# Scores of both softmax maps in one three-bank tile, and a third bank in the rotation of the other attention matmuls

## The chip, the cores and the metric

The kernel runs on one core of one Trainium2 chip. The engines named here are TensorE (PE, with its weight loads shown apart as PEld), VectorE (DVE), ScalarE (ACT), GpSimd (POOL) and SyncE (SP), whose queue issues the DMAs. Each engine takes its instructions in order; semaphores hold an instruction back until what it depends on is done. Matmul results go into accumulator tiles in PSUM. A tile of 128 x 512 f32 is called a bank here; the kernel's PSUM pools hold eight of them at any time.

The metric is the time of one execution on the device, in microseconds (us).

## The reference

Two layers of a trunk over 512 latent and 256 context tokens of width 1024. In each layer both streams are normalised and modulated, projected once into the inputs of a convolution branch, of an attention branch (q, k, v) and of two gates, merged, projected back, and passed through an MLP. What matters here is the differential attention, eight heads with two softmax maps each:

```python
def block(qi):
    s = jnp.einsum('bqhcd,bkhcd->bhcqk', qi, keys) * scale      # c: the two maps
    p = jax.nn.softmax(s, axis=-1)
    w = p[:, :, 0] - lam * p[:, :, 1]
    return jnp.einsum('bhqk,bkhv->bqhv', w, vals)
```

Latent queries (four tiles of 128 tokens) see all 768 keys. Context queries (two tiles, in the first layer only) see the 256 context keys. All products are made from operands split into a rounded part and a remainder, so that most matmuls come in threes (lines 107 to 109), and those of the scores in twos.

## The kernel before, in words

The layers run one after the other. A layer's attention loops over eight heads. While head h is attended (`attend`), the projections of head h + 1 (`qk_head`) and a share of the values of the next pair of heads (`v_pair`) are filled in between; with the last head it is the convolution's projections (`conv_a`, `conv_g`). `merge` lays the two streams out in one program order by estimated costs. The framework then sorts each engine's instructions by a timeline of its own (line 1356), so that in the trace matmuls of several steps lie among each other.

`attend` does this for each token tile t (`scores`, lines 680 to 723): for map 0 and then map 1, matmuls into a score tile S; a reduce on DVE for the row maximum (L707); an exp on ACT with that maximum as its bias (L710) into `e0` or `e1`. `e0` has two buffers, `e1` one. Then a few small instructions and L720, which combines both maps into `e0`. Later `turn` transposes the combined weights on PE (`wT`, L733) and splits them on ACT and DVE; `values` multiplies them with the values (`av`), `finish` takes the sum of squares (L758).

`qk_head` has its own steps: `project` (24 matmuls into an `mm` tile, read by an ACT copy, L537), normalisation and rotation on DVE and POOL, and `turn` (four transposes into another `mm` tile, read by L579 on ACT and by L580 and L582 on DVE). In the last layer context queries are not needed, so the context keys go another way: `ctx_keys` (kc), `ctx_norm` (kcT) and `ctx_turn` (kcD), one `mm` tile each. `v_pair` takes an `mm` tile for each of six token tiles (`v`), read by ACT and DVE (L76, L77). `conv_a` and `conv_g` take them too (`ca`, `cg`).

PSUM during attention: pool `psA` with two banks for all `mm` tiles (line 73), pool `psS` with two S tiles of two banks each (768 of 1024 columns used by a latent tile, 256 by a context tile), pool `psX` with one bank for `wT` and one for `av`. A tile takes its pool's buffers in turn, and its first writer waits until the last reader of the tile before in that buffer is done. Ahead of a layer's attention, and of the gates that follow, other pools lie in the same six banks.

Of the kernel before, what the change touches and what calls it, by code (L numbers as in the profile page):

```python
# [8 lines left out]
F32 = mybir.dt.float32  # L9
# [5 lines left out]
P = 128  # L15
# [36 lines left out]
def trunk_kernel(  # L52
# [6 lines left out]
    nc = tc.nc  # L59
    PSUM = bass.MemoryType.PSUM  # L60
# [9 lines left out]


    def mm_tile(name):
        return psA.tile([P, 512], F32, tag="mm", name=name)

    def split(hi, lo, src, lo_eng=None):
# [60 lines left out]
    rs_d = [dpool.tile([H, SEQ if i == DEPTH - 1 else NT], F32, name=f"rs_d{i}")  # L136
            for i in range(DEPTH)]

    state = {"behind": ()}
    both = nc.vector, nc.gpsimd  # L140
    first = {}

# [287 lines left out]
    for i in range(DEPTH):  # L430
# [12 lines left out]
        apool = tc.tile_pool(name=f"apool{i}", bufs=2, reuse_waits="tile")  # L443
# [230 lines left out]
        def attend(h):  # L674

            QH, QL = QKt[h]
# [3 lines left out]
            def scores(t):  # L680
                u, j = t // 2, t % 2
                lat = u < 2
                nk, kb = (NTT, 0) if lat else (2, 4)
                nkey = nk * P
                if j == 0:
# [4 lines left out]
                                     bufs=3) for tg in ("wth", "wtl")] for g in range(ng)],  # L690
                        es2=ap.tile([P, 2], F32, tag="es2", name=f"es2{i}_{h}_{u}"))
                nm = f"{i}_{h}_{t}"
                ts = slice(t * P, t * P + P)
                es = []
                st = ap.tile([P, 8], F32, tag="st", name=f"st{nm}", bufs=4)
                for m in range(2):
                    S = pS.tile([P, 768], F32, tag="S", name=f"S{nm}_{m}")
                    for lo, hi in ((0, 512), (512, 768)):
                        lo = max(lo, kb * P)
                        if hi <= lo:  # L700
                            continue
                        o = slice(lo - kb * P, hi - kb * P)
                        nc.tensor.matmul(S[:, o], QH[:, m, ts], QH[:, 2 + m, lo:hi],
                                         start=True, stop=False)
                        nc.tensor.matmul(S[:, o], QL[:, m, ts], QH[:, 2 + m, lo:hi],  # L705
                                         start=False, stop=True)
                    nc.vector.tensor_reduce(out=st[:, m : m + 1], in_=S[:, :nkey], axis=AX.X,  # L707
                                            op=ALU.max, negate=True)
                    e = ap.tile([P, 768], F32, tag=f"e{m}", name=f"e{m}{nm}", bufs=2 - m)
                    nc.scalar.activation(out=e[:, :nkey], in_=S[:, :nkey], func=AF.Exp,  # L710
                                         bias=st[:, m : m + 1],
                                         accum_out=st[:, 2 + m : 3 + m])
                    es.append(e)
# [77 lines left out]
        def spill_rstd():  # L791

            n = H * qt_n
            ps = mm_tile(f"rsT{i}")
            nc.tensor.transpose(ps[:n, :P], rsall, ident)
            row = spool.tile([P, 4, P], F32, tag="dg", name=f"rst{i}", bufs=1)[:, 0]
            nc.vector.tensor_copy(row[:n], ps[:n, :P])
            nc.sync.dma_start(rs_d[i].rearrange("h (t p) -> (h t) p", p=P), row[:n])
            yield 0.5

        def drain(gen):
            for _ in gen:
                pass
# [66 lines left out]
        turn_tile = None  # L870
        for pl in early:
            pl.__exit__(None, None, None)
        pspool = tc.tile_pool(name=f"psS{i}", bufs=2, space=PSUM, reuse_waits="tile")
        pS = pspool.__enter__()
        psx = tc.tile_pool(name=f"psX{i}", bufs=1, space=PSUM, reuse_waits="tile")
        pX = psx.__enter__()
        att_cost = 23.03 if last else 27.37
# [23 lines left out]
                main = chain_(main, rest_of(carry))  # L901
            merge(main, chain_(*fill), fc / att_cost)
        drain(spill_rstd())
        for pl in (psx, pspool, apool):
            pl.__exit__(None, None, None)


# [181 lines left out]
        for s in range(2):  # L1089
# [7 lines left out]
            for m in range(4):  # L1097
# [9 lines left out]
                for g in groups:  # L1107
                    rr[g.start] = gp.tile([P, 512], F32, tag="ar", bufs=3,
                                          name=f"mr{i}_{mb}_{g.start}")[:, : g.stop - g.start]
# [251 lines left out]
```

## Time and profile before

| | us |
|---|---|
| median of 3 runs (2361.84 to 2371.28) | 2370.24 |
| the profiled execution's time | 2368.32 |
| its span | 2366.5 |
| PE busy in the span | 2286.9 |
| first layer's attention, in the trace | 86 to 493 |
| second layer's attention, in the trace | 1440 to 1795 |

The page sorts the span of one execution by engine, by slices of time, by the chain that ended last and by groups of instructions. Matmuls are written with the tile that they make and the tiles that they read, without buffer numbers: `S<-qk` is a score matmul, `e<-S,st` an exp, `v` a values tile. "x <- y: total, times, longest" in the waits means that x's engine stood idle until y was done. The granted clock is a share of TensorE's full 2.4 GHz; its other level is 1.2 GHz.

### The profile page before, as it was taken

The page shows a single profiled execution, that of the slowest core. Times are in us where ns is not written, and L with a number is a line of the kernel's source. Part 1 is how long each engine was busy: PE and PEld are TensorE (multiplying, and loading weights), DVE is VectorE, ACT ScalarE, POOL GpSimd, SP SyncE. Part 2 cuts the span into 40 slices and gives each one's busy share as a digit, 9 for nine tenths or more (in the row PEclk, how much of TensorE's full clock was granted, in tenths as well). Part 3 has the DMA queues.
Part 4 walks back from the last instruction along what each step waited for, and adds up shares of the span by engine and source line. Part 5 has one row for each costly group of instructions (what it writes and reads, how often), then busy time and mean ns, then how long its engine had stood idle before and what let it go on. Part 6 is the DMA issues. An engine that isn't in the chain of part 4 may idle for free.

```text
span 2366.5 us, 36536 instructions
## 1 busy us (share of the span) xinstructions
PE 2286.9 (97%) x14698; PEld 2049.6 (87%) x14698; DVE 1477.9 (62%) x2581; ACT 992.1 (42%) x1965; POOL 689.4 (29%) x792
## 2 busy tenths in 40 slices
PE   7999999999999999999999998999999999999999
PEld 6999998888888988888888997999877879888887
DVE  6777776699666665555563366676759976433333
ACT  5555654522332353242514345555542333532432
POOL 2866754100000133232232365766610000000000
PEclk9999999999999999999999999999999999999999
DMA  9211111144535223334332211111123324232322
GB/s 306 60 43 35 44 45 44 46 159 135 173 114 186 84 81 124 117 115 133 108 112 85 90 55 56 43 43 41 43 76 126 129 88 127 82 97 92 104 89 71
DMA packets 222570, 224.76 MB, mean 95 GB/s; under 512 B 6256, under 2 KB 212544, under 8 KB 222272
## 3 DMA queue, kind: packets, MB, share of 16 engines
q1 hardware_dynamic: 222400, 222.43, 29.2%
q8 instruction: 115, 1.88, 0.3%
q14 instruction: 55, 0.45, 0.1%
HBM read 208.73 MB, written 13.67 MB: 94 GB/s over the span
## 4 chain that ended last, share of the span: by engine, by line
PE 81%; DVE 10%; DMA 3%; ACT 3%; POOL 2%; issue 1%; SPq 0%; ACTq 0%; DVEq 0%; POOLq 0%
PE r L107 6%; PE r L108 6%; PE r L109 6%; PE f L108 6%; PE f L107 6%; PE f L109 5%; PE gt L107 3%; PE gt L109 3%; PE gt L108 3%; PE qk L107 2%; PE qk L108 2%; PE qk L109 2%; PE v L107 2%; DVE adaac L261 2%; PE v L108 2%; PE v L109 2%
## 5 line engine op out<-in xcount | busy, mean ns | idle before, releaser
L108 PE MATMUL f<-h2l,h_w 128*128 128x512 f32 (+1 forms) x832 | 284.0, 343 | 3.8 <-DVE h2l L326 2.0
L107 PE MATMUL r<-fh,h_w 128*128 128x512 f32 (+1 forms) x832 | 283.9, 342 | 0.4 <-DVE X L1135 0.4
L107 PE MATMUL f<-h2h,h_w 128*128 128x512 f32 (+1 forms) x832 | 282.3, 343 | 2.0 <-ACT h2h L76 1.3
L108 PE MATMUL r<-fl,h_w 128*128 128x512 f32 (+1 forms) x832 | 283.2, 340 | 0.1
L109 PE MATMUL r<-fh,l_w 128*128 128x512 f32 (+1 forms) x832 | 282.9, 340 | 0.0
L109 PE MATMUL f<-h2h,l_w 128*128 128x512 f32 (+1 forms) x832 | 282.5, 341 | 0.0
L77 POOL TENSOR_TENSOR l_w<-r_w,h_w 128x1024 fp32r<-128x1024 f32 x64 | 158.1, 2492 | 348.4 <-ACT h_w L76 348.4
L261 DVE SCALAR_TENSOR_TENSOR adaac<-ar,cvec,adaac 128x256 f32<-128x256 f32 x336 | 183.0, 597 | 89.3 <-DMA ar<-in_w_ada_dram 64.2
L76 ACT ACTIVATE h_w<-r_w 128x1024 fp32r<-128x1024 f32 x128 | 128.5, 1051 | 261.5 <-PE r L108 117.2
L940 DVE SCALAR_TENSOR_TENSOR cacc<-z,cols,cacc 128x783 f32<-128x783 f32 (+1 forms) x240 | 201.1, 890 | 0.3
L107 PE MATMUL qk<-h_wqk,h1h 128*128 128x256 f32 x640 | 183.9, 289 | 5.1 <-ACT h1h L76 3.6
L108 PE MATMUL qk<-l_wqk,h1h 128*128 128x256 f32 x640 | 181.3, 285 | 0.0
L108 PEld LDWEIGHTS f<-h2l,h_w 128*128 128x128 f32 x832 | 158.3, 190 | 22.9 <-POOL h2l L77 3.0
L109 PE MATMUL qk<-h_wqk,h1l 128*128 128x256 f32 x640 | 177.1, 285 | 0.0
L107 PEld LDWEIGHTS f<-h2h,h_w 128*128 128x128 f32 x832 | 156.7, 190 | 20.6 <-ACT h2h L76 1.9
L109 PEld LDWEIGHTS f<-h2h,l_w 128*128 128x128 f32 x832 | 158.1, 190 | 17.7
L108 PEld LDWEIGHTS r<-fl,h_w 128*128 128x128 f32 x832 | 157.8, 190 | 17.5 <-DVE fl L1214 0.5
L109 PEld LDWEIGHTS r<-fh,l_w 128*128 128x128 f32 x832 | 157.6, 190 | 17.7
L107 PEld LDWEIGHTS r<-fh,h_w 128*128 128x128 f32 x832 | 157.6, 190 | 17.7 <-issue 0.5
L707 DVE TENSOR_REDUCE st<-S 128x1 f32<-128x768 f32 (+1 forms) x160 | 134.7, 846 | 61.1 <-PE S L705 60.0
L1135 DVE SCALAR_TENSOR_TENSOR X<-r,ad,X 128x512 f32<-128x512 f32 (+1 forms) x104 | 64.8, 625 | 172.8 <-PE r L109 172.5
L710 ACT ACTIVATE e<-S,st 128x768 f32<-128x768 f32 (+1 forms) x160 | 130.8, 820 | 36.3 <-DVE st L707 36.2
(253 smaller groups left out, 6245.2 us busy)
## 6 DMA issues: line engine op xcount, KB each, us to landing
r_w<-in_w_mlp_dram SPq DMA_DIRECT2D x64, 1024.0 KB, 5.5
ada<-in_w_ada_dram SPq DMA_DIRECT2D x24, 1024.0 KB, 5.8
ar<-in_w_ada_dram SPq DMA_DIRECT2D x48, 512.0 KB, 3.7
r_wqk<-in_w_in_dram SPq DMA_DIRECT2D x32, 512.0 KB, 5.2
r_wg<-in_w_in_dram SPq DMA_DIRECT2D x16, 1024.0 KB, 5.2
r_wv<-in_w_in_dram SPq DMA_DIRECT2D x8, 1024.0 KB, 5.2
r_wao<-in_w_attn_out_dram SPq DMA_DIRECT2D x8, 1024.0 KB, 5.2
r_wo<-in_w_out_dram SPq DMA_DIRECT2D x8, 1024.0 KB, 7.6
```

The costliest lines, as they stand in the source:

```text
L76: nc.scalar.activation(out=hi, in_=src, func=AF.Copy)
L77: (lo_eng or nc.vector).tensor_tensor(out=lo, in0=src, in1=f32(hi), op=ALU.subtract)
L107: nc.tensor.matmul(ps, sh, mh, start=first, stop=False)
L108: nc.tensor.matmul(ps, sh, ml, start=False, stop=False)
L109: nc.tensor.matmul(ps, sl, mh, start=False, stop=last)
L261: nc.vector.scalar_tensor_tensor(out=a[:, q], in0=r[:, j], scalar=cvec[:, k, q : q + 1], in1=a[:, q], op0=ALU.mult, op1=ALU.add)
L707: nc.vector.tensor_reduce(out=st[:, m : m + 1], in_=S[:, :nkey], axis=AX.X, op=ALU.max, negate=True)
L710: nc.scalar.activation(out=e[:, :nkey], in_=S[:, :nkey], func=AF.Exp, bias=st[:, m : m + 1], accum_out=st[:, 2 + m : 3 + m])
L940: nc.vector.scalar_tensor_tensor(out=ca[cc][:, :CV], in0=zt[cc][:, t : t + CV], scalar=wcol, in1=ca[cc][:, :CV], op0=ALU.mult, op1=ALU.add)
L1135: nc.vector.scalar_tensor_tensor(out=X[:, mb, g], in0=ps[:, :W], scalar=gate[:, s, mb : mb + 1], in1=X[:, mb, g], op0=ALU.mult, op1=ALU.add)
```

## The change

Pool `psS` has one buffer in place of two. `scores` takes one tile of 1536 columns, three banks, for both maps. For a latent tile map 0 has columns 0 to 767 and map 1 columns 768 to 1535, so the middle bank holds the end of map 0 and the beginning of map 1; map 1's matmuls are cut into 256 and 512 columns instead of 512 and 256, so that none crosses a bank. For a context tile map 0 lies in the first bank and map 1 in the third. All matmuls of both maps are written ahead of the first reduce. The reduces and exps stay as they were, each on its own columns.

The bank that this frees makes a new pool, `psB`, while a layer's attention runs. `mm_tile` counts its calls modulo 3 and takes every third tile from `psB` while that exists, the other two from `psA` as before.

```diff
     def mm_tile(name):
+        state["bank"] = (state["bank"] + 1) % 3
+        if state["bank"] == 2 and state["third"]:
+            return state["third"].tile([P, 512], F32, tag="mm", name=name)
         return psA.tile([P, 512], F32, tag="mm", name=name)
...
-    state = {"behind": ()}
+    state = {"bank": 0, "third": None, "behind": ()}
...
+                SS = pS.tile([P, 1536], F32, tag="S", name=f"S{nm}")
+                if lat:
+                    Sm = SS[:, :768], SS[:, 768:]
+                    pieces = ((0, 0, 0, 512), (0, 512, 512, 768), (1, 768, 0, 256),
+                              (1, 1024, 256, 768))
+                else:
+                    Sm = SS[:, :256], SS[:, 1024:1280]
+                    pieces = ((0, 0, 512, 768), (1, 1024, 512, 768))
+                for m, c0, lo, hi in pieces:
+                    o = SS[:, c0 : c0 + hi - lo]
+                    nc.tensor.matmul(o, QH[:, m, ts], QH[:, 2 + m, lo:hi], start=True, stop=False)
+                    nc.tensor.matmul(o, QL[:, m, ts], QH[:, 2 + m, lo:hi], start=False, stop=True)
                 for m in range(2):
-                    S = pS.tile([P, 768], F32, tag="S", name=f"S{nm}_{m}")
-                    for lo, hi in ((0, 512), (512, 768)):
-                        lo = max(lo, kb * P)
-                        if hi <= lo:
-                            continue
-                        o = slice(lo - kb * P, hi - kb * P)
-                        nc.tensor.matmul(S[:, o], QH[:, m, ts], QH[:, 2 + m, lo:hi],
-                                         start=True, stop=False)
-                        nc.tensor.matmul(S[:, o], QL[:, m, ts], QH[:, 2 + m, lo:hi],
-                                         start=False, stop=True)
+                    S = Sm[m]
                     nc.vector.tensor_reduce(out=st[:, m : m + 1], in_=S[:, :nkey], axis=AX.X,
                                             op=ALU.max, negate=True)
...
-        pspool = tc.tile_pool(name=f"psS{i}", bufs=2, space=PSUM, reuse_waits="tile")
+        pspool = tc.tile_pool(name=f"psS{i}", bufs=1, space=PSUM, reuse_waits="tile")
         pS = pspool.__enter__()
+        psthird = tc.tile_pool(name=f"psB{i}", bufs=1, space=PSUM, reuse_waits="tile")
+        state["third"] = psthird.__enter__()
...
         drain(spill_rstd())
-        for pl in (psx, pspool, apool):
+        state["third"] = None
+        for pl in (psx, psthird, pspool, apool):
             pl.__exit__(None, None, None)
```

## The prediction

> **What bounds the kernel now.** I read the page's header and its chain first, then the windows, then the waits.
>
> ```profile
> span 2366.5 us, 36536 instructions
> PE 2286.9 (97%) x14698; PEld 2049.6 (87%) x14698; DVE 1477.9 (62%) x2581; ACT 992.1 (42%) x1965; POOL 689.4 (29%) x792
> PE 81%; DVE 10%; DMA 3%; ACT 3%; POOL 2%; issue 1%; SPq 0%; ACTq 0%; DVEq 0%; POOLq 0%
> ```
>
> TensorE (PE) bounds the whole: 97% busy, 81% of the chain that ended last. The change removes no matmul, so it can only win where PE stands still or runs slowly while the two attention stretches run. The windows view gives them (columns: stretch, its us, busy us and instructions of PE, of PE's weight loads, of DVE, ACT and POOL, granted clock, DMA share, GB/s).
>
> ```profile
> 86.00:493.00 407.00, 393.23 (x2967) 373.41 (x2966) 300.18 (x573) 228.35 (x560) 225.00 (x331) 0.99 0.15 45
> 1440.00:1795.00 355.00, 331.33 (x2374) 309.77 (x2373) 247.31 (x424) 189.72 (x422) 197.00 (x272) 0.97 0.16 49
> ```
>
> Layer 0's attention (86 to 493 us) leaves PE 407.00 - 393.23 = 13.8 us idle; layer 1's (1440 to 1795) leaves 355.00 - 331.33 = 23.7 us. What PE waited for there stands in the waits view, first of layer 1's window, then of layer 0's (total us, times, longest):
>
> ```profile
> PE v L107 <- DVE qk L582: 5.9, 3, 2.5
> PE cg L107 <- ACT sg L491: 2.5, 1, 2.5
> PE v L107 <- DVE vl L77: 2.5, 1, 2.5
> PE av L758 <- ACT uo L750: 2.4, 3, 1.1
> PE qkT L575 <- DVE qk L582: 2.1, 1, 2.1
> PE S L703 <- ACT e L710: 1.9, 3, 1.4
> PE v L107 <- ACT rwc L599: 0.8, 2, 0.4
> ...
> PE S L703 <- ACT e L710: 4.7, 4, 1.8
> PE cg L107 <- ACT sg L491: 1.4, 1, 1.4
> PE ca L107 <- ACT z L476: 0.4, 1, 0.4
> PE v L107 <- DVE vl L77: 0.2, 1, 0.2
> ```
>
> Two kinds matter. A `v`, `cg`, `ca` or `qkT` matmul that waits for the reader of another tile (the values for the turned tile's last reader L582, say) needs nothing that this reader makes: it waits for one of the two `mm` banks. These are 5.9 + 2.5 + 2.5 + 2.1 + 0.8 = 13.8 us in layer 1 and 1.4 + 0.4 + 0.2 = 2.0 us in layer 0. And `S` (scores) waiting for `e` (the exp that reads an earlier score tile) is the score buffers' price today, 1.9 + 4.7 = 6.6 us.
>
> One bank wait close up, in the timelines of PE, ACT and DVE (start us, duration):
>
> ```profile
> 1584.67 0.38 PE L107 MATMUL av<-wth,vh 128*128 128x256 f32 x1 [0.35 <-ACT wth L76]
> 1587.54 0.55 PE L107 MATMUL v<-h_wv,h1h 128*128 128x256 f32 x1 [2.48 <-DVE qk L582]
> ...
> 1583.39 0.36 ACT L591 ACTIVATE kc<-kc 128x256 f32<-128x256 f32 x1
> 1583.65 0.59 ACT L579 ACTIVATE qk<-qkT 128x512 fp32r<-128x512 f32 x1
> ...
> 1586.96 0.43 DVE L582 TENSOR_TENSOR qk<-qkT,qk 64x256 fp32r<-64x256 f32 x1
> ```
>
> The `mm` tiles come in the order kc, qkT, kcT, v. With two banks v needs qkT's, whose last read ends at 1586.96 + 0.43 = 1587.39. With three it needs kc's, last read at 1583.39 + 0.36 = 1583.75, before PE even gets there (1584.7). So this wait should go whole.
>
> The stalls cost a second time. The windows view again: an undisturbed stretch, the idle spell above, then what follows it and what follows three others of layer 1:
>
> ```profile
> 1600.00:1660.00 60.00, 59.55 (x478) 57.86 (x477) 41.26 (x74) 34.20 (x79) 40.26 (x55) 1.00 0.15 43
> 1584.70:1587.60 2.90, 0.42 (x2) 0.25 (x2) 2.85 (x6) 2.37 (x6) 2.82 (x3) 0.84 0.00 0
> 1587.60:1593.50 5.90, 5.90 (x28) 5.90 (x29) 2.45 (x6) 0.00 (x0) 4.65 (x5) 0.50 0.56 177
> 1672.60:1676.50 3.90, 3.87 (x22) 3.90 (x23) 2.35 (x6) 0.00 (x0) 3.47 (x4) 0.64 0.30 93
> 1716.20:1719.80 3.60, 3.40 (x16) 3.00 (x16) 3.21 (x8) 1.55 (x4) 1.85 (x2) 0.53 0.89 289
> 1772.00:1778.00 6.00, 6.00 (x15) 4.75 (x16) 5.93 (x10) 0.60 (x1) 0.00 (x0) 0.51 0.56 178
> ```
>
> After the spells the granted clock is at or near 0.50 (the 1.2 GHz level) for some us. Undisturbed, PE starts 478 matmuls in 60 us, 8 per us. At that pace the 5.90 us with 28 would have held 47 (2.4 us lost) and the 3.90 us with 22 would have held 31 (1.2 us). The 3.60 us at 0.53 lose about half of themselves, 1.7 us, and of the 512-column matmuls, twice as long, 24 would have fitted into 6.00 us where 15 did: 2.3 us. Together 7.6 us.
>
> **The change, part by part.**
>
> *Third bank for `mm` tiles.* It adds no instruction; every third projection, value or turned tile of the attention stretch goes to it. On the table are the bank waits, 13.8 + 2.0 = 15.8 us, and the slow clock behind them, 7.6 us: bounds 0 and 23.4. I take 12 us of the waits, since the close-up shows the older bank free before PE arrives and the others are of the same shape, but a PE that comes earlier meets other waits sooner. Of the clock I take the first three stretches, 2.4 + 1.2 + 1.7 = 5.3 us; the fourth follows a spell in which `av` waited too. Late next at those places are `av` for its split weights and `kcD` for POOL's and DVE's normalisation of the context keys.
>
> *Both maps in one three-bank tile, one buffer.* The same eight matmuls a tile, the same columns (512 + 256, then 256 + 512), the same two reduces and two exps:
>
> ```profile
> L707 DVE TENSOR_REDUCE st<-S x160: 412/948/961, 91.1 to 1755.8; 128x1 f32<-128x768 f32 x128, 128x1 f32<-128x256 f32 x32
> L710 ACT ACTIVATE e<-S,st x160: 464/902/976, 92.1 to 1761.2; 128x768 f32<-128x768 f32 x128, 128x256 f32<-128x256 f32 x32
> ...
> 1450.79 0.90 ACT L710 ACTIVATE e<-S,st 128x768 f32<-128x768 f32 x1 [0.49 <-DVE st L707]
> 1451.00 0.95 DVE L707 TENSOR_REDUCE st<-S 128x1 f32<-128x768 f32 x1
> ```
>
> Three waits are new. First, map 0's reduce waits for the matmuls that put map 1's first 256 columns beside it in the middle bank: two of them at 60 / 478 us, 0.25 us. Second, map 1's reduce reads the bank that map 0's exp reads. Today they overlap, as the last two rows show (0.90 us from 1450.79, 0.95 us from 1451.00, two tiles). Whether such reads are kept apart when they share a bank, no row shows. The nearest is `av L758 <- ACT uo L750` above: a matmul into columns 256 and 257 waits for a read of columns 0 to 255 of its bank that makes nothing it needs. I take it that they are kept apart: bounds 0 and 128 / 2 x 0.95 = 61 us, were every one on the path. Third, the next token tile's scores wait for the second exp, where today each map follows its own.
>
> The Trainium skill, page "PSUM — Partial Sum Buffer", section "Terms", says that two engines on one bank and quadrant at once are an error, reads against reads included. By it the second wait is certain, and the sum with all of it exposed would be 61 us worse; the overlap in the rows is of different banks and does not contradict it. The sum below does not use it.
>
> What hides all this is time between tiles. The new cycle of a latent tile is 1.5 us of matmuls (four of 0.125 us, four twice as wide), then 0.95 + 0.90 + 0.95 + 0.90, some 5.2 us and queueing. Layer 0 gives a tile 407 / 48 = 8.5 us, layer 1 355 / 32 = 11.1 us, and a context tile (412 ns, 464 ns) needs half. Nor is S what holds the exp back in layer 0. From one late tile of a head (DVE, ACT, then PE):
>
> ```profile
> 153.60 0.95 DVE L707 TENSOR_REDUCE st<-S 128x1 f32<-128x768 f32 x1
> 159.35 1.48 DVE L720 SCALAR_TENSOR_TENSOR e<-e,st,e 128x768 f32<-128x768 f32 x1
> ...
> 157.90 0.90 ACT L710 ACTIVATE e<-S,st 128x768 f32<-128x768 f32 x1
> ...
> 156.99 0.49 PE L733 MATMUL wT<-cst,e 128*128 128x128 f32 x3
> ...
> 169.41 0.49 PE L733 MATMUL wT<-cst,e 128*128 128x128 f32 x3
> ```
>
> The reduce ends at 154.55, its exp starts at 157.90, 0.42 us after the transposes of the tile two before (156.99 + 0.49 = 157.48) free its `e0` buffer. That is 3.3 us of slack ahead of the exp; and the combination ends at 160.83 (159.35 + 1.48) while the tile's first transposes come at 169.41, 8.6 us later. A second reduce and exp behind the first (1.85 us) fits into either. I charge 3 us for more S waits; bounds: today's 6.6 us gone, or the 61 us, plus 64 x 0.90 = 58 us of exps, exposed.
>
> *The rest.* The first score tile needs three freed banks of the earlier pools instead of two; other projections fill PE there, cost nothing, 4 us were that cover gone. No DMA, SP or POOL instruction is added or moved by the source; the order within each engine is sorted anew, which I can't price and count as some 5 us either way.
>
> **Sum.** -12 - 5.3 + 3 = -14.3 us. Against the profiled execution's 2368.3 us (span 2366.5) that is 2354; the three runs have a median of 2370.24, so 2356 on their scale.
>
> **Rivals.**
> 1. *Given back.* The bank waits go, but PE meets the next wait (weights of `av`, POOL's doubled tiles) or `S <- e` doubles to 13 us: about -15.8 + 10 to 15 with the clock unimproved, 2364 to 2369. For it: layer 0 has little to win (2.0 us). Against: the longest waits are whole idle spells with only the bank missing. A counter that handed out an occupied third bank while another is free would end here too.
> 2. *Slower.* The serial cycle S, reduce, exp, reduce, exp becomes layer 0's pace. Place: latent tiles of layer 0, 32 of them. Price: 1.85 us each behind the first exp, 59 us, of which some 4 us a head (the 3.3 us before an exp, once) stay hidden: 59 - 32 = 27 us, plus 8 us as PE idles and loses its clock, less the 17 us won: 2388. It decides once queueing on DVE (busy 300 of 407 us) and ACT lifts the 5.2 us cycle past 8.5 us. For it: DVE is the busiest helper there. Against: the slack measured above.
>
> **How the numbers follow.** 0.5% of 2370.24 is 11.9 us, about what a measurement of this kernel can tell from no change. Forecast 0.50 (2344 to 2358: from all 23.4 us won and some of today's S waits gone, to barely the 12). Given back 0.28 (2358 to 2382). Slower 0.22 (around 2388). So faster 0.50, same 0.28, slower 0.22. The range goes down to 2340 (all 23.4 us won and all 6.6 us of S waits gone) and up to 2384, which takes in both first cases and leaves out most of the third.
>
> **What would show it.** Right: `v <- qk L582`, `v <- vl` and `cg <- sg` nearly gone from layer 1's waits; no half-clock stretch near the head boundaries; PE busy share of layer 1's attention above 96%; `S <- e` at 5 to 12 us in all; the second reduce of a latent tile always after the first exp. Wrong: `S <- e` above 20 us, or layer 0's attention longer than 407 us with idle PE; the first means that the cycle paces, the second that the sorting found worse orders. If the reduce still overlaps the exp, my second wait was never there.

## The result, and the profile after

| | us |
|---|---|
| before, 9 runs beside the changed kernel (2361.84 to 2373.92) | 2366.92 |
| changed, 9 runs (2371.96 to 2378.89) | 2375.24 |
| ratio | 1.0033, 95% interval 1.0022 to 1.0044 |

The changed kernel takes 8 us more. That is less than the 0.5% that was counted as no change, but it is clear of the noise, since the interval doesn't reach 1. The forecast had 14 us less. First the header of the page and the chain of the changed kernel.

```profile
span 2373.5 us, 36456 instructions
PE 2283.3 (96%) x14698; PEld 2046.3 (86%) x14698; DVE 1484.5 (63%) x2581; ACT 997.6 (42%) x1965; POOL 671.7 (28%) x792
PE 84%; DVE 6%; ACT 3%; POOL 3%; DMA 2%; issue 1%; SPq 0%; ACTq 0%; DVEq 0%; POOLq 0%
```

The same 14698 matmuls, about the same busy time, and 7 us more of span: PE waits more. Below, "attention" is the time from the start of a layer's first score matmul to the start of its `rsT` matmul, which closes it. It was 402.9 us in layer 0 and 353.8 in layer 1; now it is 411.5 and 364.2. That is 8.6 and 10.4 us, of which 12 come back outside these stretches, as part of the other work has moved inside (PE is busy 4.3 and 3.9 us longer in the windows below than in the prediction's). The windows view of both layers, changed kernel:

```profile
86.00:501.00 415.00, 397.55 (x2975) 375.20 (x2975) 304.31 (x566) 232.47 (x559) 215.28 (x331) 0.99 0.15 44
1436.00:1803.00 367.00, 335.24 (x2410) 314.54 (x2409) 253.29 (x431) 194.05 (x427) 195.68 (x275) 0.95 0.17 52
```

PE idles 17.5 us in layer 0 (13.8 before) and 31.8 in layer 1 (23.7). The waits of PE in the changed kernel, layer 1 first (window 1436 to 1803), then layer 0 (86 to 501); every line number behind the scores is 8 higher now, those of `qk` and `kc` 3.

```profile
PE kcT L600 <- ACT kc L594: 11.3, 6, 2.2
PE av L111 <- DVE wtl L80: 4.7, 1, 4.7
PE S L711 <- ACT e L718: 4.6, 2, 4.1
PE rsT L803 <- POOL rsall L773: 4.4, 1, 4.4
PE cg L110 <- ACT sg L494: 2.5, 1, 2.5
...
PE wT L741 <- DVE wtl L80: 4.3, 7, 1.2
PE av L110 <- ACT wth L79: 2.2, 4, 0.8
PE S L711 <- ACT e L718: 2.2, 3, 1.7
PE qk L110 <- DVE qk L585: 1.8, 2, 0.9
```

The bank waits of layer 1 that the change was to remove (`v <- qk`, `v <- vl`, `qkT <- qk`) are gone, all but the 2.5 us of `cg`. In their place stand `kcT`, which waits for its own operand, the copied context keys, and two long waits, for `wtl` and `rsall`, at the end of the last head. In the kernel before the three had little (window 1440 to 1795):

```profile
PE rsT L795 <- POOL rsall L765: 1.9, 1, 1.9
...
PE av L108 <- DVE wtl L77: 0.6, 1, 0.6
PE kcT L597 <- ACT kc L591: 0.5, 1, 0.5
```

Waiting for scores, `S <- e`, was 1.9 us in layer 1 and 4.7 in layer 0 and is 4.6 and 2.2: the same in sum. From this table alone the one score buffer costs nothing. The experiments say otherwise.

One latent tile in layer 0, from the timelines of PE, DVE and ACT of the changed kernel: its first and last score matmul, both reduces and exps, and the first score matmul of the next tile.

```profile
235.88 0.48 PE L711 MATMUL S<-qk 128*128 128x512 f32 x1
...
237.13 0.39 PE L712 MATMUL S<-qk 128*128 128x512 f32 x1
...
237.83 0.95 DVE L715 TENSOR_REDUCE st<-S 128x1 f32<-128x768 f32 x1
238.81 0.90 ACT L718 ACTIVATE e<-S,st 128x768 f32<-128x768 f32 x1 [1.85 <-DVE st L715]
239.61 0.19 ACT L718 ACTIVATION_READ_ACCUMULATOR e<-S,st 128x1 f32 x1
239.84 0.96 DVE L715 TENSOR_REDUCE st<-S 128x1 f32<-128x768 f32 x1 [1.06 <-ACT e L718]
240.83 0.90 ACT L718 ACTIVATE e<-S,st 128x768 f32<-128x768 f32 x1 [0.32 <-DVE st L715]
241.63 0.19 ACT L718 ACTIVATION_READ_ACCUMULATOR e<-S,st 128x1 f32 x1
...
243.96 0.40 PE L711 MATMUL S<-qk 128*128 128x512 f32 x1
```

From the first score matmul to the end of the second exp (240.83 + 0.90 = 241.73) the tile is held for 5.9 us even here, where hardly anything queues, and PE comes to the next one 2.2 us later, since other matmuls stand ahead in its order: 8.1 us a tile. Over layer 0's 32 latent tiles the means are 6.7 us held and 2.3 us until the next tile's scores, 9.0 together. The time from one latent tile's second exp to the next one's within a head (24 pairs a layer) says it without a model: 7.45 us before and 8.87 now in layer 0, 8.61 and 10.27 in layer 1. Context tiles and the turn of the head give part of it back, 8.20 us a step before and 7.14 now in layer 0.

The second reduce (239.84) starts when the first exp's last part has ended (239.61 + 0.19 = 239.80). It does so in all 80 tiles; before, 25 of 80 overlapped. The Trainium skill, page "PSUM — Partial Sum Buffer", section "Terms", counts two engines on the same bank and quadrant at once as an error, reads against reads included, and the order of the reduces is in line with it. But the rows don't show that the shared bank is the reason: e4 and e11 below, which give each map a bank of its own in the one tile, have the same order in all 80 tiles.

### The profile page after: what moved, and what is told of

The parts are those of the page before. It is cut to its first block, busy times and chain, and to the rows that moved or that the text cites. A ratio compares the mean times of both kernels' runs of the same rounds, so it can differ in the third digit from the quotient of the medians.

```text
span 2373.5 us, 36456 instructions
## 1 busy us (share of the span) xinstructions
PE 2283.3 (96%) x14698; PEld 2046.3 (86%) x14698; DVE 1484.5 (63%) x2581; ACT 997.6 (42%) x1965; POOL 671.7 (28%) x792
## 4 chain that ended last, share of the span: by engine, by line
PE 84%; DVE 6%; ACT 3%; POOL 3%; DMA 2%; issue 1%; SPq 0%; ACTq 0%; DVEq 0%; POOLq 0%
PE r L110 6%; PE r L111 6%; PE r L112 6%; PE f L111 6%; PE f L110 6%; PE f L112 6%; PE gt L110 3%; PE gt L112 3%; PE gt L111 3%; PE qk L110 3%; PE qk L111 3%; PE qk L112 2%; PE S L711 2%; PE S L712 2%; PE v L110 2%; PE o L112 2%
```

## The experiments

The expectations speak of four theories. **1:** one score buffer makes the chain of scores, reduces and exps late. **2:** the second reduce, which waits for the first exp, does. **3:** three `mm` banks by themselves give worse orders. **4**, formed after the first four runs: the third bank lets the fill (projections, values, convolution) run ahead of the attention chain, which is then left with nothing beside it. The lead of the fill can be counted: at each token tile's first score matmul, how many fill matmuls are done beyond those that stand ahead of it in program order. In layer 0 it is mostly 24 before (at most some 70), and up to 168 in the changed kernel.

Most of them, with attention by layer in the trace and the ratio to the kernel before, measured beside it (two layers with different settings are written layer 0 / layer 1). Where S has two buffers with own banks, a buffer holds one map; elsewhere a buffer holds both:

| kernel | S: buffers, maps | `mm` banks in layer 0 / 1 | layer 0 | layer 1 | ratio |
|---|---|---|---|---|---|
| before | 2, own banks | 2 / 2 | 402.9 | 353.8 | |
| changed | 1, shared | 3 / 3 | 411.5 | 364.2 | 1.0033 |
| e2 (control) | 2, own, cut | 2 / 2 | 403.4 | 352.4 | 0.9984 |
| e3 | 2, own, cut | 3 / 3 | 422.8 | 348.8 | 1.0027 |
| e4 | 1, own, cut | 3 / 3 | 413.3 | 363.8 | 1.0026 |
| e5 | 2, shared, cut | 3 / 3 | 413.6 | 358.7 | 1.0028 |
| e1 | 1, shared | 2 / 2 | 415.9 | 384.9 | 1.0192 |
| e11 | 1, own, cut | 2 / 2 | 415.7 | 385.5 | 1.0166 |
| e12 | 2, shared, cut | 2 / 2 | 400.0 | 364.1 | 1.0026 |
| e6 | 2, own, cut | 2 / 3 | 403.3 | 349.2 | 0.9966 |
| e7 | 2, own, cut | 2 / 3, not last head | 403.4 | 346.8 | 0.9945 |
| e10 | before's / changed | 2 / 3 | 403.4 | 355.0 | 0.9959 |
| e8 | before's / changed | 2 / 3, not last head | 403.2 | 348.6 | 0.9948 |
| e15 | changed / before's | 3 / 2 | 410.9 | 358.8 | 1.0053 |
| e14 | 1, shared | 3 / 3, not last heads | 416.6 | 354.4 | 1.0037 |

### Taking the change apart, on scores cut to one bank

To try the parts separately there must be free banks. In the control each map's scores go into one bank: the second piece is written over the first 256 columns, and reduce and exp read these three times, so instructions and sizes stay and the attention isn't the reference's.

```diff
-                    S = pS.tile([P, 768], F32, tag="S", name=f"S{nm}_{m}")
+                    S = pS.tile([P, 512], F32, tag="S", name=f"S{nm}_{m}")
...
-                        o = slice(lo - kb * P, hi - kb * P)
+                        o = slice(0, hi - lo)
...
+                    S3 = S[:, :256].unsqueeze(1).to_broadcast([P, nkey // 256, 256])
```

> A control for the three runs beside it. The kernel before, with each score tile cut to one bank: the second piece of a latent tile's scores is written over the first 256 columns, and reduce and exp read these 256 columns three times, so that all instructions keep their counts and sizes while two of the eight banks are left unused. The output is not the reference's. Every theory expects the time of before, 2362 to 2373 us, and the first layer's attention to end (rsT) near 489 us. If it does not, the three others are to be read against this one.

Measured 0.9984 (0.9973 to 0.9995): a control that stands within 4 us of the kernel before, with its attention. Now the third `mm` bank alone (e3), the one buffer with a bank for each map (e4), and two buffers with both maps in one bank (e5), the last two with the third bank too.

e3 adds `mm_tile`'s counter and the pool `psB` of the changed kernel to the control, nothing else:

```diff
+        state["bank"] = (state["bank"] + 1) % 3
+        if state["bank"] == 2 and state["third"]:
+            return state["third"].tile([P, 512], F32, tag="mm", name=name)
```

e4's and e5's score tiles, in this order, against the changed kernel's; pool `psS` keeps one buffer in e4 and has two in e5:

```diff
-                SS = pS.tile([P, 1536], F32, tag="S", name=f"S{nm}")
+                SS = pS.tile([P, 1024], F32, tag="S", name=f"S{nm}")
+                Sm = SS[:, :256], SS[:, 512:768]
```

```diff
-                SS = pS.tile([P, 1536], F32, tag="S", name=f"S{nm}")
+                SS = pS.tile([P, 512], F32, tag="S", name=f"S{nm}")
+                Sm = SS[:, :256], SS[:, 256:512]
```

> The control plus the third mm bank, scores as before (two buffers, a map at a time). The output is not the reference's. Theory 1 (the third bank wins in the fill, and the one score buffer makes the chain of scores, reduces and exps late, which shows at the last head, where no fill is left): 2350 to 2360 us, the projections of the second layer earlier than in before by some 8 us at the last head, and the attention's ends (rsT) not later than in the control. Theory 2 (the loss is the second reduce that waits for the first exp): the same. Theory 3 (three mm banks by themselves make worse orders: the wait of kcT for kc, 11 us in the changed kernel, takes the place of the bank waits): 2365 to 2375 us, with kcT <- kc near 11 us.

> The changed kernel with a score tile of two banks in place of three, a bank for each map (scores cut as in the control): still one buffer for both maps, still three mm banks, but no bank that both maps share. The output is not the reference's. Theory 1: the one buffer is the cost, so as the changed kernel, 2370 to 2380 us, rsT some 8 to 10 us later than in before in both layers. Theory 2: as the run with three mm banks and scores as before, 2350 to 2360 us, the second reduce overlapping the first exp in some 25 tiles. If the second reduce still never overlaps the first exp, the order is kept for the whole tile and not by bank, and this run says nothing on theory 2.

> The changed kernel with both maps in one single bank and two such buffers, three mm banks (scores cut as in the control): the second reduce must wait for the first exp in every tile, but the next token tile's scores no longer wait for this tile's second exp. The output is not the reference's. Theory 1: the one buffer was the cost, so near the run with three mm banks and scores as before, 2350 to 2362 us, rsT at most 3 us later than in the control. Theory 2: as the changed kernel, 2370 to 2380 us, rsT 8 to 10 us later.

Measured 1.0027 (1.0013 to 1.0040), 1.0026 (1.0012 to 1.0039) and 1.0028 (1.0015 to 1.0040): the same loss three times, with the score tile changed or not. So the third bank, which was to win, loses 0.4% by itself against the control (1.0027 / 0.9984), in layer 0 (422.8 us against 403.4) more than it wins in layer 1. Theories 1 and 2 seemed to fall. They had only been asked in the company of three banks.

### The score tile without the third bank

e1 is the changed kernel with the third bank never handed out; e11 and e12 are e4 and e5 with the same edit.

```diff
-        state["third"] = psthird.__enter__()
+        psthird.__enter__()
```

> The changed kernel with the third mm bank left unused: both maps in the one three-bank score tile, projections, values and turned tiles in two banks as before. Theory 4 (run-ahead: the third mm bank lets projections, values and conv work run ahead of the attention chain, so that the chain's last head ends with nothing beside it): fill stays close to the chain, the tail of layer 1's last head loses about 9 us of PE as before and not 22, bank waits of 10 to 16 us are back in layer 1, total ratio 0.998 to 1.001. Rival, the score tile is what costs (second reduce behind the first exp, one buffer): ratio 1.003 or more, with the tail as in the changed kernel.

Measured 1.0192 (1.0166 to 1.0218), 2410.9 us. That is 45 us, on the rival's side and far beyond its 1.003: 13 us lie in layer 0's attention and 31 in layer 1's. Nor do 10 us of bank waits come back, as theory 4 had it: the waits of e1's layer 1 (window 1449 to 1835) are mostly those of late softmax weights.

```profile
PE av L110 <- ACT wth L79: 10.0, 5, 2.5
PE wT L741 <- DVE wtl L80: 9.5, 4, 3.2
PE kcT L600 <- ACT kc L594: 6.6, 5, 2.5
PE av L111 <- DVE wtl L80: 6.5, 2, 4.6
```

Which property of the tile costs this?

> As e4_one_buffer_own_banks (both maps in one tile with one buffer, but each map in a bank of its own; each map's scores cut to one bank as in the control, so the attention is not the reference's), with two mm banks as before. e1_two_mm showed that the score tile without the third bank costs some 45 us. If the single buffer (the next tile's scores wait for both maps' exps) is what costs, this comes out near e1: ratio 1.014 or more, layer 0's attention 413 us or more, layer 1's 378 or more. If the shared bank is (the second reduce behind the first exp, the first reduce behind the second map's matmuls), it comes out near the control: ratio 1.004 or less.

> As e5_two_buffers_one_bank (both maps' cut scores in one bank, two buffers; the attention is not the reference's), with two mm banks as before. If the shared bank is what costs in e1_two_mm: ratio 1.014 or more. If the single buffer is: near the control, ratio 0.998 to 1.004, layer 0's attention 403 to 407 us and layer 1's 352 to 358.

One buffer with own banks (e11): 1.0166 (1.0143 to 1.0190), against the control 1.82%, 43 us, and both layers' attention within 0.6 us of e1's. So it makes no difference whether the maps share a bank. The second reduce's wait, however, is still there. In e11, as in e4, it comes behind the first exp in all 80 tiles, here in the timelines of DVE and ACT:

```profile
215.61 0.95 DVE L715 TENSOR_REDUCE st<-S 128x1 f32<-128x768 f32 x1
217.62 0.96 DVE L715 TENSOR_REDUCE st<-S 128x1 f32<-128x768 f32 x1 [1.06 <-ACT e L718]
...
216.59 0.90 ACT L718 ACTIVATE e<-S,st 128x768 f32<-128x768 f32 x1 [2.88 <-DVE st L715]
217.39 0.19 ACT L718 ACTIVATION_READ_ACCUMULATOR e<-S,st 128x1 f32 x1
```

This is the case in which, by e4's expectation, the run says nothing on theory 2, and e11 doesn't either.

Two buffers with a shared bank (e12), where the second reduce waits for the first exp in all 80 tiles as well: 1.0026 (1.0015 to 1.0037), against the control 0.4%, 10 us, in layer 1 alone (364.1). So with both maps joined in one tile and a **single buffer** the loss is 43 us, and a second buffer takes 33 of them back (1.0166 / 1.0026). Most of it is theory 1: there is no room for the next tile while this one is held. Two things remain open. e12 has room for two whole tiles, where the control's two buffers hold one map each and come free one by one. And the second reduce's wait makes the hold longer; what the single buffer would cost without it, no run shows, since every kernel with both maps in one tile has it (e9 below puts another wait in its place).

The steps between latent tiles within a head agree: in layer 0 they take 7.45 us in the control, 7.63 in e12 and 8.66 in e11. But they take 8.40 in e3 too, with the old scores and the third bank, so the changed kernel's 8.87 alone doesn't tell the single buffer from the third bank.

The loss shows as `wT` and `av` that wait, not as `S <- e`: the sorting puts other matmuls where the scores would stand and wait (e17 below takes these away).

> As e8_real_layer2, with both maps' reduces written ahead of both exps in layer 1, so that the second reduce need not wait for the first exp. If the reduce that waits for the exp in the shared bank still costs in layer 1: 1 to 4 us less than e8 (2351 to 2354 on e8's scale of 2355.3). If that wait lies beside other work: within 1 us of e8, or anywhere within 3 us by another order.

```diff
-                    nc.vector.tensor_reduce(out=st[:, m : m + 1], in_=S[:, :nkey], axis=AX.X,
-                                            op=ALU.max, negate=True)
+                    if m == 0 or not Sm:
+                        for q in range(2) if Sm else (m,):
+                            nc.vector.tensor_reduce(out=st[:, q : q + 1],
+                                                    in_=(Sm[q] if Sm else S)[:, :nkey],
+                                                    axis=AX.X, op=ALU.max, negate=True)
```

A miss: 1.0032 (1.0018 to 1.0046), some 20 us worse than e8 (below), layer 1's attention 372.7 us. The first exp now comes behind the second reduce, on the mean 1.90 us after the first reduce's end where e8 has 0.91, and the order around them came out worse. So it takes the second reduce's wait away and puts another in its place, and doesn't settle what the first one costs.

### The third bank by layers, and the last head

e6 is e3 with the bank in the second layer only (`last`); e7 adds the second edit below, in the loop over heads.

```diff
-        state["third"] = psthird.__enter__()
+        pB = psthird.__enter__()
+        state["third"] = pB if last else None
```

```diff
+            if h == H - 1:
+                state["third"] = None
```

> Kernel e3_one_bank_three_mm with the third mm bank in layer 1 (the second layer) only; the scores of each map are cut to one bank (second piece over the first 256 columns, reduce and exp read these 256 columns three times, so the attention is not the reference's). Theory 4: layer 0's attention is back at the control's length, 403 us (e3: 423), layer 1's stays near e3's 349, total near 2356 to 2363, ratio to the control about 0.997. Rival (the orders are drawn anew by any change, nothing is tied to the third bank's layer): layer 0 as the control, layer 1 anywhere within 349 to 360.

> As e6_third_in_layer2 (same cut scores), and in layer 1's last head the third mm bank is given up again, so that what is left of projections and values there goes by two banks. Theory 4: PE's loss in the last head's tail falls from some 21 us back towards the control's 9, layer 1's attention 338 to 343 us, total 2346 to 2354. Rival (the fill ran ahead in the heads before, so that giving up the bank in the last head is too late, or the tail's loss has nothing to do with it): the tail loses 18 us or more as in e6, total equal to e6 within 3 us.

e6 came out as theory 4 expected: layer 0 403.3, layer 1 349.2, ratio 0.9966 (0.9953 to 0.9980). e7 won another 5 us, 2352.4 (0.9945, 0.9927 to 0.9962), though its layer 1 (346.8) didn't reach the 338 to 343. Against the control the bank is worth 0.9966 / 0.9984, 4 us, and without the last head 0.9945 / 0.9984, 9 us.

Why the last head? The windows view of the last 40 us before `rsT` in layer 1, first the kernel before, then the changed one (columns as in the prediction).

```profile
1753.20:1793.20 40.00, 32.41 (x158) 26.65 (x157) 27.87 (x44) 14.64 (x28) 7.02 (x6) 0.89 0.19 60
```

```profile
1760.60:1800.60 40.00, 24.64 (x120) 20.10 (x119) 29.39 (x46) 14.09 (x27) 9.62 (x6) 0.79 0.20 64
```

PE does 24.6 us of work there instead of 32.4, at a lower granted clock. The timelines of the changed kernel's DVE, PE and POOL show what the chain's last steps wait for:

```profile
1787.47 2.35 DVE L80 TENSOR_TENSOR l_wg<-r_wg,h_wg 128x1024 fp32r<-128x1024 f32 x2
1789.74 0.74 DVE L951 SCALAR_TENSOR_TENSOR cacc<-z,cols,cacc 128x512 f32<-128x512 f32 x1
1790.40 0.68 DVE L496 TENSOR_TENSOR z<-z,sg 128x512 f32<-128x512 f32 x1
1791.00 0.74 DVE L951 SCALAR_TENSOR_TENSOR cacc<-z,cols,cacc 128x512 f32<-128x512 f32 x1
1791.66 0.55 DVE L80 TENSOR_TENSOR wtl<-wT,wth 128x384 fp32r<-128x384 f32 x1
...
1792.27 0.58 PE L111 MATMUL av<-wtl,vh 128*128 128x256 f32 x1 [4.68 <-DVE wtl L80]
...
1793.91 6.04 DVE L951 SCALAR_TENSOR_TENSOR cacc<-z,cols,cacc 128x512 f32<-128x512 f32 x9
...
1796.78 3.73 POOL L773 TENSOR_TENSOR rsall<-rsall,mhalf 128x2 f32<-128x2 f32 x1 [23.11 <-ACT rsall L770]
1800.57 0.39 PE L803 MATMUL rsT<-cst,rsall 128*32 128x128 f32 x1 [4.38 <-POOL rsall L773]
```

In the last head the fill is the convolution's projections. Done earlier, they hand DVE the gating (`z`), taps (`cacc`) and the next weights' split (`l_wg`) earlier: four us of it (1787.47 to 1791.66) stand ahead of the last `wtl`, and PE, with no fill left, waits 4.68 us for it; then the power on POOL lies beside a run of taps and takes 3.73 us.

### On the real kernel

e8 has the kernel before in layer 0 and the changed one in layer 1, without the third bank in the last head; e10 keeps it there; e15 is the counterpart, changed in layer 0 alone; e14 is the changed kernel without the third bank in either last head. Against the kernel before, without the code of the scores, which is chosen by the same `last`:

```diff
-        pspool = tc.tile_pool(name=f"psS{i}", bufs=2, space=PSUM, reuse_waits="tile")
+        pspool = tc.tile_pool(name=f"psS{i}", bufs=1 if last else 2, space=PSUM, reuse_waits="tile")
...
+        if last:
+            psthird = tc.tile_pool(name=f"psB{i}", bufs=1, space=PSUM, reuse_waits="tile")
+            state["third"] = psthird.__enter__()
...
+            if h == H - 1:
+                state["third"] = None
```

e10 is without the last two lines; e14 is the changed kernel with only these two.

> Layer 0 as in the kernel before (four score banks, two mm banks), layer 1 as in the changed kernel (three score banks in one tile, three mm banks) but with the third mm bank given up in the last head. Theory 4: layer 0's attention 403 us, layer 1's 350 to 356 (changed: 364), total 2356 to 2366. Rival (layer 1's loss comes from the single score tile): layer 1's attention stays at 360 to 365, total 2366 to 2374.

> As e8_real_layer2 (layer 0 as before, layer 1 as in the changed kernel), but the third mm bank stays in use in the last head, as in the changed kernel. Tells apart where e8's gain in layer 1 (348.6 us against 364.2) comes from. Theory 4 (run-ahead costs the last head's tail): the tail loses some 20 us as in the changed kernel, layer 1's attention 356 to 364, total 2360 to 2368. Rival (layer 1 is better in e8 because of how the first layer leaves it, the last head is not what counts): layer 1's attention within 3 us of 348.6, total within 4 us of e8.

> Layer 0 as in the changed kernel (one three-bank score tile, three mm banks), layer 1 as before. The counterpart of e10_real_layer2_kept (layer 0 as before, layer 1 as changed: 2361.7, layer 1's attention 355.0 where the changed kernel has 364.2). If the two layers' parts add up: layer 0's attention 411 to 412 us, layer 1's 352 to 355, total 2373 to 2378. If what layer 0's change does reaches into layer 1 by the sorting (which the 9 us between e10 and the changed kernel suggest): layer 1's attention 358 us or more, total above 2379.

> The changed kernel with one edit: in the last head of both layers the third mm bank is no longer used. If the tails of the two last heads hold the loss because the fill ran ahead of the chain (theory 4): layer 0's tail (12.4 us of PE in the changed kernel, 6.7 before) and layer 1's (20.6, before 7.1) fall, total 2359 to 2369. Rival (the changed kernel's order is worse all along, the single buffer being the cause everywhere): total within 4 us of the changed kernel's 2375.

e8 takes 2355.3 us, 0.9948 (0.9932 to 0.9964), and beats the kernel before by 0.5%; layer 1's attention is 348.6 us. e10, with the bank in the last head, 2361.7 (0.9959, 0.9942 to 0.9975) and 355.0. The last 40 us, e10 and then e8:

```profile
1747.50:1787.50 40.00, 24.20 (x118) 19.77 (x117) 29.02 (x45) 13.82 (x27) 9.65 (x6) 0.79 0.20 64
```

```profile
1742.00:1782.00 40.00, 32.32 (x166) 26.68 (x164) 30.18 (x46) 17.53 (x33) 7.88 (x8) 0.96 0.18 60
```

PE's 8 us of work in this stretch come and go with the last head's third bank; layer 1's attention differs by 6.4 us. In the whole time it shows between e6 and e7 (5.6 us, each run of e7 below each of e6), but not between e8 and e10, whose ratios lie 0.11% apart, inside their intervals. e14 has the same stretch as e8 in layer 1:

```profile
1757.40:1797.40 40.00, 32.59 (x162) 26.75 (x161) 29.86 (x46) 17.25 (x32) 7.46 (x7) 0.91 0.19 60
```

Its layer 1 is 10 us shorter than the changed kernel's (354.4). But layer 0 is 5 us longer (416.6), perhaps because the fill stands far ahead when the bank goes; in all 2375.0 us, 1.0037 (1.0025 to 1.0048), nothing won. Theory 4 held for one layer and missed in the other.

e15, changed in layer 0 alone, takes 2379.0 us, 1.0053 (1.0035 to 1.0071). So layer 0's share of the change costs some 12 us (8 of them in its own attention, and 5 in that of layer 1, 358.8 from 353.8, although its source is the one before), layer 1's wins 10 (e10), and together +0.53 - 0.41 = +0.12%, where +0.33% was measured. The rest, 5 us, is put down to the sorting, which is not shown by a run of its own: layer 1 of the changed kernel has the source of e10's and takes 9 us more. Why, stays open.

> The same kernel as e8_real_layer2 with more rounds, as the version that beats both kernels: median 2355.3 there, ratio 0.9948. Expected: ratio 0.993 to 0.997, layer 0's attention 403 us, layer 1's 348 to 350.

Measured 2354.2 us, 0.9944 (0.9929 to 0.9960), layer 0 403.3 and layer 1 346.6: the gain of e8 is there again.

> As e8_real_layer2, but layer 1 takes its three-bank score tile from the pool only once and writes all token tiles' scores into it, so that a score matmul waits for the readers of the columns or the bank that it writes, not for the release of the whole tile. If the release of the whole tile after the second exp is what the single buffer costs in layer 1: 2 to 6 us less than e8, 2349 to 2353. If not, or if the middle bank makes it wait as long: within 3 us of e8, or a few us more by another order.

```diff
-                    SS = pS.tile([P, 1536], F32, tag="S", name=f"S{nm}")
+                    if "SS" not in state:
+                        state["SS"] = pS.tile([P, 1536], F32, tag="S", name=f"S{nm}")
+                    SS = state["SS"]
```

2354.0 us (0.9952, 0.9934 to 0.9969): as e8. But no score matmul of layer 1 came earlier for it: in e16 as in e8 each first one starts at least 0.14 us after the second exp of the tile before has ended. So the run doesn't tell what a release by parts would be worth.

### Is the run-ahead the cause in layer 0, or the cover?

On the changed kernel, with nothing else altered, each fill matmul of both attention stretches is put behind the score matmuls ahead of it in program order (e17), or behind those of the tile before the last (e18, with 2 in place of 1 in the first line below). That sets layer 0's lead to 0, and to mostly 24 to 48.

```diff
+                    for ins in state["sc"][-1:][:1] if len(state["sc"]) >= 1 else ():
+                        es.enter_context(tc.issue_after(ins))
+                    c_ = next(fill, None)
```

> The changed kernel with an order added on TensorE alone: in both layers' attention each fill matmul (projections, values, conv) is queued behind the score matmuls ahead of it in program order, so that the fill's lead, up to 168 matmuls in the changed kernel's layer 0, is 0 everywhere. If the run-ahead itself is what costs (theory 4): layer 0's attention 400 to 405 us where the changed kernel has 411.5, the tail of layer 1's last head back to some 10 us, total 2355 to 2367. Rival (the run-ahead only follows from the single buffer, whose scores come free too late, and covers it): PE waits for the scores instead, layer 0 over 415 us, total above 2380.

> As e17_fill_held_1, but behind the scores of the token tile before the last: the lead in layer 0 is 24 to 48 matmuls, as in the kernel before (0 to 72). Theory 4: layer 0's attention 402 to 406 us, total 2360 to 2368, and no more waiting for scores than in the changed kernel. Rival: total within 4 us of the changed kernel's 2375, or slower.

Theory 4 falls in layer 0. e17: 2408.3 us, 1.0179 (1.0159 to 1.0198), layer 0's attention 443.4 us. e18: 2377.8 us, 1.0049 (1.0032 to 1.0067), layer 0 409.1, 2 us shorter than the changed kernel's and no cheaper in all. Waits of PE in e17's layer 0 (window 89 to 534), then in e18's (88 to 500):

```profile
PE S L712 <- ACT e L720: 15.7, 19, 1.9
PE wT L743 <- DVE wtl L80: 10.2, 9, 1.6
```

```profile
PE S L712 <- ACT e L720: 5.0, 7, 1.1
```

With the fill held in place PE stands 15.7 us before the scores, as the one buffer has it; the changed kernel's 2.2 us are low because the fill has gone ahead instead. So in layer 0 the run-ahead is cover for the single buffer, not the cause of the loss.

It doesn't need the third bank. Counted against e17's order, layer 0's lead is 24 at the median in the kernel before and 0 in e12, but 93 (up to 144) in e1 and e11, which have two `mm` banks, and 120 in the changed kernel. Nor does the third bank win much there: of the 36 us from e1 to the changed kernel 4 lie in layer 0's attention and 21 in layer 1's. In layer 1 e1's fill stands some 28 matmuls behind e17's at the median, the changed kernel's level with it. There the joined tile with one buffer costs little beside the third bank: e8's attention takes 348.6 us, and 346.8 in e7, which has the old tiles with cut scores.

Not tried: holding the fill back in e3, where the third bank alone, with the old scores, makes layer 0 19 us longer and the lead grows to some 160 as well. What costs there isn't settled, and theory 3 isn't excluded for it; nor was a second buffer for the real three-bank tile tried, since six banks for scores and two for `wT` and `av` leave none for `mm`.

## Why the prediction was wrong

- **"What hides all this is time between tiles ... I charge 3 us for more S waits"** is the step that failed. The new cycle was put at "some 5.2 us and queueing" against 8.5 us a tile in layer 0 and 11.1 in layer 1. In layer 0 it measures 6.7 us held and 2.3 until PE takes it up, 9.0: the sum of durations left out the accumulator reads (0.19 us a map), the hops between engines (0.35 us on the mean from the last score matmul to the reduce) and PE's own queue ahead of the next scores. And 8.5 us was the mean over latent and context tiles; latent tiles within a head followed each other at 7.45 us. In layer 1 it is 7.8 and 2.8 us, 10.5, where latent tiles within a head had followed each other at 8.61. The cover wasn't 3.3 us a tile, it was none. Without the third bank the score tile costs 45 us where 3 were charged (e1); on cut scores it is 43 (e11), of which a second buffer takes 33 back (e12).
- **The sum** took the two parts as independent, and they are not. The third bank alone, with the old scores, costs 10 us against the control (e3); the score tile alone costs 45; together they cost 8.
- **The slack measured** (3.3 us before an exp, 8.6 us before the transposes) was read from one late tile of a head, held up by its `e0` buffer, and said nothing of the tiles ahead of it.
- **The second wait**, the reduce behind the first exp, is there, as taken, but also where the maps have a bank each (e11), so a shared bank isn't needed for it. Together with the first wait it costs 10 us where there are two buffers (e12 against e2); beside the single buffer its price isn't shown apart.
- **-12 and -5.3 us for the third bank.** Mechanism right for the waits of layer 1: the bank waits named are gone but for `cg`, and e7 wins 9 us with two score buffers and the third bank there. Size off by two things that the part didn't look at: in the last head the bank brings DVE's convolution work forward, and PE does 8 us less in the last 40 us (e10 against e8); in layer 0, where 2 us were to be had, the third bank alone makes the attention 19 us longer (e3). The 5.3 us of clock didn't come: PE idles more, and layer 1's mean granted clock is 0.95 from 0.97. Stretches at the half clock (0.50, the 1.2 GHz level) stand elsewhere now, again around idle spells; three of them:

```profile
1448.00:1451.00 3.00, 2.39 (x8) 2.10 (x9) 1.66 (x3) 0.56 (x2) 2.92 (x5) 0.50 0.03 5
1775.00:1778.00 3.00, 1.70 (x4) 1.41 (x5) 1.65 (x3) 1.83 (x3) 0.00 (x0) 0.50 0.03 5
1792.30:1801.00 8.70, 3.49 (x14) 3.11 (x15) 7.65 (x12) 1.16 (x4) 3.73 (x1) 0.50 0.54 172
```

- **"The order ... I can't price and count as some 5 us either way"** was too small: the same source in layer 1 came out 9 us apart (e10 and the changed kernel), and e9 some 20.
- **Rival 1**, given back, names the outcome: PE meets the next wait (`kcT`, `av`, `rsT`), and layer 0 has little to win. But that the net is small is luck: it is what is left of 45 us lost by the score tile and some 36 won back by the bank beside it (e1). **Rival 2** names the cause, the serial cycle: in layer 0 it stands past the 8.5 us at which it was to decide (9.0), and latent tiles follow each other at 8.87 us from 7.45. But its place was layer 0, and without the third bank layer 1 loses more (31 of e1's 45 us). Its 2388 us stand between e1's 2411 and the changed kernel's 2375.
- **What would show it:** the waits of `v` gone, the second reduce behind the first exp, `S <- e` at 5 to 12 us (6.8) came true. `cg <- sg` stayed at 2.5 us, the half-clock stretches stayed, and PE's share above 96% in layer 1 did not come (335.24 of 367.00, 91%). Of the signs of being wrong, layer 0 is longer than 407 us, which the prediction put down to worse orders, while `S <- e`, its sign for the cycle, stayed low. `S <- e` was the wrong sign to watch: sorted ahead of time, the loss shows at the operations behind it.

## What to carry to other kernels

Compare a buffer's cycle (held, plus the time until its engine takes it up again, both from rows) with the spacing of the very steps that use it, not with a mean over lighter ones; if the two are close, as here, room for a second tile can be worth far more than a bank for other work: 33 us here (e11 to e12). Where a scheduler fills the waiting engine with other work, a wait's total isn't its price: pin the order, or take the cover away, and it shows. A bank given to filler work is worth taking back where the filler's readers share an engine with the last steps of the chain: here 5.6 us (e6 to e7).

## What had not been expected of the hardware

The power of two elements on POOL (`rsall`, L765 before, L773 after) takes 0.73 us in the middle of layer 1 and 1.28 at its end before:

```profile
1479.16 0.73 POOL L765 TENSOR_TENSOR rsall<-rsall,mhalf 128x2 f32<-128x2 f32 x1 [7.27 <-ACT rsall L762]
...
1791.84 1.28 POOL L765 TENSOR_TENSOR rsall<-rsall,mhalf 128x2 f32<-128x2 f32 x1 [20.17 <-ACT rsall L762]
```

After, it is the 3.73 us shown above, beside nine taps of DVE, each with two operands beside its scalar. In all traces together 19 of these powers took over 2.5 us (3.39 to 5.09), and every one lay at least 0.84 of its time beside DVE's work, taps above all. Lying beside taps isn't enough, though: at 468.46 in the kernel before one took 1.44 us with 0.98 of it beside taps. The Trainium skill, page "SBUF — State Buffer", section "SBUF: two separate sides", says that GpSimd and a VectorE instruction with two SBUF inputs take a shared pair of ports one at a time. The long powers fit it, but no run took the taps away from a power that is otherwise the same, so it is argued and not shown. It is worth 2.5 us in layer 1 (`rsT`'s wait, 4.4 us from 1.9), at a place where PE has nothing else to do.
